# The row factor of an RMSNorm moved behind the up projection, with splits made tile by tile and up weights combined in place

## The chip, the cores and the metric

The kernel runs on one core of a Trainium2 chip. The metric is the device time of one execution in microseconds (us). The engines are named as in the profile: PE (TensorE matmul), PEld (its weight loads), DVE (VectorE), ACT (ScalarE), POOL (GpSimd) and SP (SyncE, which here only issues DMAs).

## The reference, cut to what matters

The model is a two-layer decoder trunk over 1032 rows (1024 of a prompt, 8 samples) with 1024 columns. Each layer adds a mixer's output through an output projection and then a convolutional FFN:

```python
x = x + jnp.concatenate([main, mo], axis=-1) @ prm['w_out'][l]
hn = _rmsnorm(x, prm['norm_ffn_g'][l])          # x * r * g, r one number per row
u = hn @ prm['w_ffn_up'][l]                     # 1024 -> 2 * 3072
u, nbuf = _causal_dwconv(u, buf, cw, cb)        # width 3, per channel
x = x + (jax.nn.gelu(u[..., :D_FF]) * u[..., D_FF:]) @ prm['w_ffn_down'][l]
```

All is float32. The row factor `r` is one number per row of `x`, so it can be applied to `hn` or, as well, to the rows of `u`.

## The kernel before, in words

Activations lie transposed: channels on the 128 partitions, the 1032 rows of the model along the free dimension. `row()` gives one tile of 128 x 1032 from a pool of 44, `sm()` one of 128 x 392 from a pool of 12. Every matrix product is done as three matmuls (`mm3`) on operands split in a high part (`fp32r`, copied by ACT) and the rest (a subtraction on POOL or DVE). So each weight and each activation is split before PE can use it. The order of ACT's instructions is the program's from the start up to the first layer's end and again in the last FFN (`act_in_order`); DVE, POOL, PE and SP are ordered by the compiler's scheduler. DMAs are all issued by SP, whose queue runs in order.

**Output projection** (`out_proj`). The 1032 columns are two halves of 516, each half two quarters of 258 (`QB`, `QW`). For each half the loop goes over the 8 output tiles `m`; each takes a split weight tile (`get`, one split ahead, one load ahead), loads the residual tile `x[m]` (first half), runs 2 x 24 matmuls, adds the result to `x[m]` on DVE, stores it to `rD` (SP), squares it on ACT and sums the squares on DVE (`on_tile`). Background work is a list of generators; `tick()` advances each by one step.

**Entry to the FFN** (`enter_ffn`). After each half `norm(hf)` computes the row factor (`inverse`: a matmul with ones, Ln and Exp on ACT, a correction step on DVE), multiplies every quarter of `x` by factor and gain (`scale`), and forms and splits the seven operands of a seven-product scheme (`B11`, `B21`, `B22`, `T1` to `T4`). The last half's `norm` runs after the last tile of the projection, and the products that follow need its results.

**Up projection** (`ffn`). For each of 24 channel pairs `j` there are seven products (`STEADY`), each 24 matmuls (12 for each half), with the weight combination made by `combine`, up to five products ahead: for a pair it makes 4 sums or differences of 128 x 512 and 7 splits of 128 x 512 on POOL, and 7 copies on ACT. Two of the sums stand in a row of their own (`S`). `load_pair(j + 1)` is asked for at the pair's first combination. ACT or DVE adds each product into the rows `ug`, `uv`. `post(j)` then makes the convolution: an ACT instruction (`act_conv`), two DVE taps for each row, an addition of 8 sample columns for each row (`taps`), a gelu on ACT and a product on DVE, and a store to `gD`.

**Down projection.** It reads `gD` back, splits and multiplies; `refill` reads `x` back from `rD`.

Of the kernel before, what the change touches and what calls it, by code (L numbers as in the profile page):

```python
# [36 lines left out]
DCH = 6  # L37
NDC = KF // DCH
# [4 lines left out]
STEADY = ("P1", "P6", "P2", "P7", "P5", "P4", "P3")  # L43
ENTRY = tuple((0, p, (0,)) for p in STEADY) + tuple((0, p, (1,)) for p in ("P1", "P2", "P6", "P7", "P5", "P4", "P3"))
SEQUENCE = ENTRY + tuple((j, p, (0, 1)) for j in range(1, KF) for p in STEADY)
ORDER_A = ("g2", "g3", "x0", "x1", "x2", "x3", "x4", "x5", "g4", "g5")
# [3 lines left out]
def tile_trunk(ctx: ExitStack, tc: tile.TileContext, I: dict, O: list):  # L50
# [502 lines left out]
    def unspill(k):  # L553
        t = row()
        SY.dma_start(t[:, :SEQ].rearrange("p (i t) -> p i t", i=8), xD[0:8, :, k, :].rearrange("i p t -> p i t"))
        SY.dma_start(t[:, SEQ:NT], xD[8, :, k, :NB])
        return t
# [132 lines left out]
    def sample_mem(l, dst):  # L690
# [35 lines left out]
        yield  # L726
        t = ps()
# [40 lines left out]
    def residual(l, m):  # L768
        if l:
            return unspill(m)  # L770
        t = row()
        SY.dma_start(t[:, :NT], I["x_t"][:, m, :])
        return t

    def out_proj(l, mget, ks, x, on_tile, on_half):
        for hb in range(2):
            for m in range(KD):
# [4 lines left out]
                for q in (2 * hb, 2 * hb + 1):  # L782
                    c0 = QB[q]
# [15 lines left out]
    def ffn_prep(l):  # L799
# [11 lines left out]
        vtt(s3, s3, c3, add)  # L811

    def up_weights(l):
# [10 lines left out]
        def combine(j, name):  # L824
            R = raws[j]
            lo_, hi_ = slice(0, 512), slice(512, 1024)
            if name == "P1":
                if j:
                    load_pair(j + 1)
                src = R["G"][:, lo_]  # L830
            elif name == "P6":
                S = R["S"] = row()
                gtt(S[:, lo_], R["V"][:, lo_], R["V"][:, hi_], add)
                gtt(S[:, hi_], S[:, lo_], R["G"][:, lo_], sub)
                src = S[:, hi_]
            elif name == "P2":
                src = R["G"][:, hi_]
            elif name == "P7":
                src = R["G"][:, lo_]
                gtt(src, src, R["V"][:, lo_], sub)  # L840
            elif name == "P5":
                src = R["S"][:, lo_]
            elif name == "P4":
                src = R["V"][:, hi_]
            else:
                src = R["S"][:, hi_]
                gtt(src, R["G"][:, hi_], src, sub)
# [4 lines left out]
            R["n"] = R.get("n", 0) + 1  # L852
            if R["n"] == 7:
                raws[j] = None
# [3 lines left out]
    def ffn(l, x, ops, need, weights, on_block, store=None):  # L858
# [5 lines left out]
        def act_conv(u, t):  # L864
            a = row()
            act(a[:, :NT], u[:, :NT], AF.Identity, scale=fwc(2, t), bias=fbc(t))
            G.tensor_copy(out=ul3[:, :, t], in_=u[:, SEQ - 2 : NT])
            return a

        def taps(a, u, t):  # L870
            stt(a[:, 1:SEQ], u[:, 0 : SEQ - 1], fwc(1, t), a[:, 1:SEQ], mul, add)
            stt(a[:, 2:SEQ], u[:, 0 : SEQ - 2], fwc(0, t), a[:, 2:SEQ], mul, add)
            vtt(a[:, SEQ:NT], a[:, SEQ:NT], sb3[:, :, t], add)

        def post(j):
# [9 lines left out]
            act(ag[:, :NT], ag[:, :NT], AF.Gelu_apprx_tanh)  # L885
            yield
            vtt(ag[:, :NT], ag[:, :NT], av[:, :NT], mul)
            SY.dma_start(gD[l, j], ag[:, :NT])
            yield

# [61 lines left out]

        last = []
        todo = [(0, p) for p in STEADY] + [(j, p) for j, p, _ in SEQUENCE if j]
        at = 7
        for q, (j, name, hfs) in enumerate(SEQUENCE):
            if q == 6:
                load_pair(1)
            want = 7 if q < 10 else min(len(todo), q - 7 + AHEAD)
# [51 lines left out]
        for b in range(3):  # L1011
            for m in range(KD):
                down(c, m, b)
                if store is not None:
                    store(m, b)
                tick()
            on_block(b)
# [269 lines left out]
    SY.dma_start(O[1], yl)  # L1287
    SY.dma_start(O[2], rl)
# [21 lines left out]
    def enter_ffn(l, x, mh, ml):  # L1310
        ops, gen, sums = {}, {}, {}

        def split(name, kk, hf, pair, raw, on_pool):
            hi, lo = pair
            acopy(hi, raw)
            (gtt if on_pool else vtt)(lo, raw, f(hi), sub)
            ops[name, kk, hf] = pair

        def cols(q):
            return slice(QB[q], QB[q] + QW)  # L1320

        def on_tile(q, m):
            SY.dma_start(rD[l, m, :, cols(q)], x[m][:, cols(q)])
            if m == 0:
                sums[q] = sm()
                act(sums[q][:, :QW], x[m][:, cols(q)], AF.Square)
            else:
                t = sm()
                act(t[:, :QW], x[m][:, cols(q)], AF.Square)
                vtt(sums[q][:, :QW], sums[q][:, :QW], t[:, :QW], add)  # L1330

        def inverse(q):
            a = sums.pop(q)
            p = ps()
            T.matmul(p[:, :QW], ones, a[:, :QW], start=True, stop=True)
            m, out, t = sm()[:, :QW], sm()[:, :QW], sm()[:, :QW]
            ts(V, m, p[:, :QW], 1.0 / D, EPS, mul, add)
            act(out, m, AF.Ln)
            act(out, out, AF.Exp, scale=-0.5)
            stt(t, m, -0.5, out, mul, mul)  # L1340
            vtt(t, t, out, mul)
            stt(out, t, 1.5, out, add, mul)
            return out

        def norm(hf):
            qa, qb = cols(2 * hf), cols(2 * hf + 1)
            ra, rb = inverse(2 * hf), inverse(2 * hf + 1)
            yield
            xs = lambda k, part: x[k][:, part]

            def scale(k, part, r):
                stt(xs(k, part), xs(k, part), g_ffn[l][k], r, mul, mul)

            def slot(k, part):
                return mh[k][:, part], ml[k][:, part]

            def own(n):
                for i in range(n):
                    if i % 2 == 0:
                        t = row(F32R)  # L1360
                    b = (i % 2) * 2 * QW
                    yield t[:, b : b + QW], t[:, b + QW : b + 2 * QW]

            for k in range(KD):
                scale(k, qa, ra)
                split("B11" if k < 4 else "B21", k % 4, hf, slot(k, qa), xs(k, qa), k % 2)
                if k % 4 == 3:
                    yield
            t2 = own(4)
            for kk in range(4):  # L1370
                scale(kk, qb, rb)
                scale(kk + 4, qb, rb)
                vtt(xs(kk, qa), xs(kk, qb), xs(kk, qa), sub)
                vtt(xs(kk, qb), xs(kk + 4, qb), xs(kk, qb), sub)
                split("B22", kk, hf, slot(kk + 4, qb), xs(kk + 4, qb), True)
                vtt(xs(kk + 4, qb), xs(kk + 4, qb), xs(kk, qa), sub)
                split("T2", kk, hf, next(t2), xs(kk + 4, qb), False)
                if kk % 2:
                    yield
            t2 = own(4)  # L1380
            for kk in range(4):
                split("T3", kk, hf, next(t2), xs(kk, qb), kk % 2)
            yield
            for kk in range(4):
                split("T1", kk, hf, slot(kk, qb), xs(kk, qa), kk % 2)
                if hf:
                    x[kk] = None
            yield
            t2 = own(4)
            for kk in range(4):  # L1390
                vtt(xs(kk + 4, qa), xs(kk + 4, qa), xs(kk + 4, qb), sub)
                split("T4", kk, hf, next(t2), xs(kk + 4, qa), kk % 2)
                if hf:
                    x[kk + 4] = None
            yield
# [3 lines left out]
        def first_pair():  # L1399
# [3 lines left out]
            yield  # L1403
            for name in STEADY:
                weights[1](0, name)
                yield

        def on_half(hf):
            if hf:
                finish(gen["w"])  # L1410
            gen[hf] = start(norm(hf))
            if not hf:
                gen["w"] = spawn(first_pair())
# [5 lines left out]
        return on_tile, on_half, need, ops, weights  # L1419
# [5 lines left out]

    x = [None] * KD
    ot, oh, need, ops, uw = enter_ffn(0, x, Mh, Ml)
    out_proj(0, mgetA, ks_a, x, ot, oh)
    Mh, Ml = {}, {}

# [52 lines left out]
    def handB(b, x=x):  # L1483
# [30 lines left out]
    ffn(0, x, ops, need, uw, handB)  # L1514
# [333 lines left out]
    x = [None] * KD  # L1848
# [5 lines left out]
    ot, oh, need, ops, uw = enter_ffn(1, x, Mh, Ml)  # L1854
# [3 lines left out]
    def y_out(m, b, x=x):  # L1858
# [133 lines left out]
```

## Time and profile before

| | |
|---|---|
| median of three runs | 2533.51 us (2530.58 to 2537.18) |
| profiled execution, its own time | 2532.97 us |
| its span in the trace | 2531.2 us |
| PE busy | 2336.5 us (92%) |
| mean granted TensorE clock | 0.964 of full |

The span is what lies between the first and the last recorded instruction; 1.8 us of the profiled execution's time lie around it. "Busy" of an engine includes time in which an instruction has begun and waits inside (for a port). Wait lists say which engine or DMA ended an idle time.

### The profile page before, as it was taken

To read this page: it belongs to the slowest core of one execution; us is meant where nothing else is said; L and a number is where in the kernel's file an instruction comes from. 1 tells how busy PE (TensorE), PEld (TensorE's weight loads), DVE (VectorE), ACT (ScalarE), POOL (GpSimd) and SP (SyncE) were. 2 spreads that over 40 slices of the span, in tenths; PEclk is the share of its full clock that TensorE was granted. 3 is DMA by queue.
4 is the path that set the end of the run, shared out by engine and by line. 5 is a ranking of instruction groups with operands and counts; after the bars stand their busy time and mean duration, and the time that the engine had idled before them with its cause. 6 is when DMAs were issued, how large, how long until landed. Compare 5 with 4: busy or idle time off the path is not lost. (4 is left out here: it accounts for less than half of the span.)

```text
span 2531.2 us, 42857 instructions
## 1 busy us (share of the span) xinstructions
PE 2336.5 (92%) x16590; PEld 2251.5 (89%) x16590; DVE 1549.6 (61%) x2826; ACT 1103.5 (44%) x2277; POOL 1428.0 (56%) x1123
## 2 busy tenths in 40 slices
PE   7997877799999999999989988787999999999999
PEld 5896866799999999999977787677999999999999
DVE  6658955666666666332478789875666566663321
ACT  5567753344433444211365577643443444442110
POOL 2149843588888885322144346435888888853220
PEclk9998989899999999999999999899999999999999
DMA  4221124212222225421575543551222222253311
GB/s 163 87 69 56 58 83 143 63 67 84 84 85 76 76 76 199 150 95 52 178 252 162 185 152 129 163 157 63 77 86 82 76 76 76 76 224 123 101 55 63
DMA packets 142491, 273.64 MB, mean 108 GB/s; under 512 B 28544, under 2 KB 85456, under 8 KB 142288
## 3 DMA queue, kind: packets, MB, share of 16 engines
q1 hardware_dynamic: 142288, 270.91, 31.9%
q8 instruction: 130, 2.13, 0.3%
q14 instruction: 73, 0.60, 0.1%
HBM read 211.99 MB, written 58.87 MB: 107 GB/s over the span
## 5 line engine op out<-in xcount | busy, mean ns | idle before, releaser
L116 POOL TENSOR_TENSOR row<-row,row 128x512 fp32r<-128x512 f32 (+9 forms) x754 | 1153.8, 1552 | 793.9 <-ACT row L105 476.4
L298 PE MATMUL ps<-row,row 128*128 128x258 f32 (+4 forms) x5032 | 1510.4, 303 | 55.5 <-ACT row L105 45.7
L299 PE MATMUL ps<-row,row 128*128 128x258 f32 (+4 forms) x5032 | 1509.1, 302 | 22.5 <-DVE row L113 18.7
L300 PE MATMUL ps<-row,row 128*128 128x258 f32 (+4 forms) x5032 | 1472.7, 301 | 23.5 <-POOL row L116 23.5
L298 PEld LDWEIGHTS ps<-row,row 128*128 128x128 f32 x5032 | 962.3, 191 | 73.9 <-ACT row L105 51.0
L299 PEld LDWEIGHTS ps<-row,row 128*128 128x128 f32 x5032 | 964.0, 192 | 40.2 <-DVE row L113 24.3
L300 PEld LDWEIGHTS ps<-row,row 128*128 128x128 f32 x5032 | 948.4, 192 | 34.1 <-POOL row L116 27.1
L105 ACT ACTIVATE row<-row 128x512 fp32r<-128x512 f32 (+8 forms) x768 | 505.4, 696 | 911.7 <-POOL row L116 305.4
L113 DVE TENSOR_TENSOR row<-row,ps 128x258 f32<-128x258 f32 (+2 forms) x736 | 322.3, 444 | 706.0 <-PE ps L300 666.5
L119 DVE SCALAR_TENSOR_TENSOR row<-row,fw,row 128x1023 f32<-128x1023 f32 x192 | 266.9, 1409 | 67.3 <-ACT row L105 67.3
L113 DVE TENSOR_TENSOR row<-row,row 128x258 fp32r<-128x258 f32 (+8 forms) x262 | 232.9, 912 | 31.3 <-ACT row L105 18.0
L105 ACT ACTIVATE row<-ps 128x258 f32<-128x258 f32 (+6 forms) x430 | 157.5, 406 | 69.6 <-PE ps L300 25.8
L116 POOL TENSOR_TENSOR row<-row,ty 128x768 f32<-128x768 f32 (+2 forms) x56 | 77.2, 1378 | 155.1 <-DVE ty L413 51.3
L105 ACT ACTIVATE row<-row,fw 128x1032 f32<-128x1032 f32 x96 | 114.9, 1245 | 68.8 <-DVE row L113 68.7
L105 ACT ACTIVATE sm<-row 128x258 f32<-128x258 f32 (+3 forms) x130 | 54.5, 452 | 153.5 <-DVE row L113 127.2
L113 DVE TENSOR_TENSOR row<-row,sb 128x8 f32<-128x8 f32 x96 | 102.3, 1066 | 0.0
L113 DVE TENSOR_TENSOR sm<-sm,sm 128x258 f32<-128x258 f32 (+5 forms) x125 | 81.9, 660 | 28.2 <-ACT sm L105 25.7
L105 ACT ACTIVATE row<-ps,ty,ty 128x256 f32<-128x256 f32 (+1 forms) x160 | 87.4, 564 | 10.1 <-DVE ty L113 7.6
L105 ACT ACTIVATE sm<-ps 128x384 f32<-128x384 f32 (+5 forms) x156 | 65.0, 444 | 39.2 <-PE ps L431 21.6
L113 DVE TENSOR_TENSOR row<-ps,row 128x384 fp32r<-128x384 f32 (+2 forms) x125 | 63.5, 519 | 25.1 <-ACT row L105 10.2
L119 DVE SCALAR_TENSOR_TENSOR row<-sm,pack,row 128x384 f32<-128x384 f32 (+1 forms) x54 | 62.6, 1162 | 14.6 <-POOL row L124 13.3
L116 POOL TENSOR_TENSOR sm<-sm,row 128x192 f32<-128x192 f32 (+3 forms) x72 | 49.5, 702 | 36.1 <-ACT sm L105 18.6
(163 smaller groups left out, 1497.3 us busy)
## 6 DMA issues: line engine op xcount, KB each, us to landing
row<-in_w_ffn_up SPq DMA_DIRECT2D x96, 512.0 KB, 3.3
gD<-row SPq DMA_DIRECT2D x48, 516.0 KB, 2.6
row<-gD SPq DMA_DIRECT2D x48, 516.0 KB, 5.6
row<-in_w_ffn_down SPq DMA_DIRECT2D x64, 384.0 KB, 3.1
row<-hD SPq DMA_DIRECT2D x48, 512.0 KB, 6.6
row<-in_w_out SPq DMA_DIRECT2D x32, 512.0 KB, 4.2
rD<-row SPq DMA_DIRECT2D x64, 129.0 KB, 1.9
row<-rD SPq DMA_DIRECT2D x16, 516.0 KB, 8.7
```

The source lines that it names most:

```text
L105: return nc.scalar.activation(out, in_, func, **kw)
L113: return V.tensor_tensor(out=out, in0=a, in1=b, op=op)
L116: return G.tensor_tensor(out=out, in0=a, in1=b, op=op)
L119: return V.scalar_tensor_tensor(out=out, in0=a, scalar=s, in1=b, op0=op0, op1=op1)
L298: T.matmul(out, ah, bh, start=first and j == 0, stop=False, skip_group_check=more)
L299: T.matmul(out, ah, bl, start=False, stop=False, skip_group_check=more)
L300: T.matmul(out, al, bh, start=False, stop=last and j == n - 1, skip_group_check=more)
```

## The change

- `out_proj` goes over the tiles in the order 0, 4, 1, 5, ... (`TILES`), and residual tiles hold a half of two channel tiles; they are asked for ahead of the loop and then one for each of the first four tiles of a half.
- `on_tile` adds on DVE into a small tile, copies that times the gain into `x` on ACT, and stores the small tile to `rD` by a DMA issued on ACT's queue. The sums and splits of `T2`, `T3`, `T4` (`combine_x`) are made after every second tile; `settle` splits `B11` with `T1`, and `B21` with `B22`, as rows of 516.
- The row factor is not applied there. `factor()` makes one row `rf` in the middle of the first products, and `act_conv` multiplies each finished row `ug`, `uv` (128 x 1032) by it on DVE, 96 times in all.
- The 8 sample columns leave `taps`; `samples` treats them for 12 pairs at a time, with POOL, and stores them apart.
- `combine` works in the raw weight rows in the order `PREPARED`; the row `S` is gone; the next pair is asked for at `P4`, the sixth of seven. The first pair's combinations begin in the first half of the projection.
- Two small outputs are stored after the projection of layer 0 instead of ahead of it, and the sample attention over memory has two more `yield`s between its softmax and its transposes.

```diff
-            for m in range(KD):
+            for m in TILES:
                 key = f"out{l}.{hb}.{m}"
                 wh, wl = get(key, 1, 1)
-                if x[m] is None:
-                    x[m] = residual(l, m)
+                if m < 4:
+                    fetch()
...
-                    vtt(x[m][:, c0 : c0 + QW], x[m][:, c0 : c0 + QW], p[:, :QW], add)
-                    on_tile(q, m)
+                    on_tile(hb, part, m, p[:, :QW])
...
         def combine(j, name):
-            if name == "P1":
-                if j:
-                    load_pair(j + 1)
-                src = R["G"][:, lo_]
+            if name == "P1":
+                src = G[:, lo_]
+            elif name == "P7":
+                src = G[:, lo_]
+                gtt(src, src, V_[:, lo_], sub)
             elif name == "P6":
-                S = R["S"] = row()
-                gtt(S[:, lo_], R["V"][:, lo_], R["V"][:, hi_], add)
-                gtt(S[:, hi_], S[:, lo_], R["G"][:, lo_], sub)
-                src = S[:, hi_]
+                src = G[:, lo_]
+                gtt(src, V_[:, hi_], src, sub)
...
+            if name == "P4" and j:
+                load_pair(j + 1)
...
         def act_conv(u, t):
+            vtt(u[:, :NT], u[:, :NT], factor()[:, :NT], mul)
             a = row()
-            act(a[:, :NT], u[:, :NT], AF.Identity, scale=fwc(2, t), bias=fbc(t))
+            act(a[:, :SEQ], u[:, :SEQ], AF.Identity, scale=fwc(2, t), bias=fbc(t))
...
         def taps(a, u, t):
-            vtt(a[:, SEQ:NT], a[:, SEQ:NT], sb3[:, :, t], add)
...
+        def on_tile(hf, part, m, p):
+            q = 2 * hf + part
+            xs, t = place(hf, part, m), sm()
+            vtt(t[:, :QW], xs, p, add)
+            acopy(xs, t[:, :QW], scale=g_ffn[l][m])
+            nc.scalar.dma_start(rD[l, m, :, QB[q] : QB[q] + QW], t[:, :QW])
...
+        def combine_x(hf, kk):
+            a, b = place(hf, 0, kk), place(hf, 1, kk)
+            c, d = place(hf, 0, kk + 4), place(hf, 1, kk + 4)
+            t3, t2, t4 = (sm()[:, :QW] for _ in range(3))
+            vtt(t3, d, b, sub)
+            vtt(b, b, a, sub)
+            vtt(t2, d, b, sub)
+            vtt(t4, c, t2, sub)
...
+        def settle(hf):
+            cs = slice(hf * HALF, hf * HALF + HALF)
             for kk in range(4):
+                for a, names in enumerate((("B11", "T1"), ("B21", "B22"))):
+                    k = kk + 4 * a
+                    hi, lo, raw = mh[k][:, cs], ml[k][:, cs], x[hf, kk][:, a * HALF : a * HALF + HALF]
+                    acopy(hi, raw)
+                    (gtt if a else vtt)(lo, raw, f(hi), sub)
```

## Rows read from the trace of the kernel before

**Rows 1.** The page: busy time of each engine over the span.
```profile
PE 2336.5 (92%) x16590; PEld 2251.5 (89%) x16590; DVE 1549.6 (61%) x2826; ACT 1103.5 (44%) x2277; POOL 1428.0 (56%) x1123
```

**Rows 2.** Windows: two projection-and-entry stretches, one up-projection slice, layer 0's up projection.
```profile
347.20:522.40 175.20, 132.05 (x926) 125.18 (x927) 98.98 (x187) 61.90 (x142) 85.00 (x67) 0.87 0.33 106
1660.00:1785.80 125.80, 98.02 (x696) 92.33 (x695) 83.36 (x170) 49.09 (x117) 63.81 (x57) 0.88 0.27 85
...
700.00:800.00 100.00, 100.00 (x835) 100.00 (x834) 63.88 (x85) 42.06 (x70) 85.08 (x65) 1.00 0.23 80
...
523.00:985.00 462.00, 459.65 (x3819) 459.06 (x3818) 297.90 (x390) 195.25 (x322) 389.88 (x295) 1.00 0.23 82
```

**Rows 3.** PE's waits, 345 to 523 us: total, times, longest.
```profile
PE ps L298 <- ACT row L105: 20.1, 9, 8.2
PE ps L300 <- POOL row L116: 12.4, 9, 2.0
```

**Rows 4.** SP's queue in time: start, us, line, transfer.
```profile
344.77 0.34 SPq L1287 DMA_DIRECT2D out<-yl  x1
...
366.67 0.80 SPq L1323 DMA_DIRECT2D rD<-row  x2
...
1671.54 32.45 SPq L1323 DMA_DIRECT2D rD<-row  x10
1704.09 0.37 SPq L251 DMA_DIRECT2D row<-in_w_out  x1
```

**Rows 5.** DVE's waits, 345 to 412 us.
```profile
DVE row L113 <- DMA row<-in_x_t: 37.4, 7, 6.0
```

**Rows 6.** Groups of the whole kernel by shape: one POOL split, the scaling on DVE.
```profile
L116 POOL TENSOR_TENSOR row<-row,row 128x1024 fp32r<-128x1024 f32 x46 | 114.7, 2495 | 110.8 <-ACT row L105 92.3 <-issue 13.4 <-DMA rD<-row 5.1
...
L119 DVE SCALAR_TENSOR_TENSOR row<-row,pack,sm 128x258 f32<-128x258 f32 x64 | 39.2, 672 | 0.2
```

**Rows 7.** PE's waits, 200 to 345 us: the longest.
```profile
PE ps L729 <- DVE sm L123: 12.6, 1, 12.6
```

**Rows 8.** POOL's groups by shape, 600 to 900 us, fifteen pairs.
```profile
L116 POOL TENSOR_TENSOR row<-row,row 128x512 fp32r<-128x512 f32 x105 | 165.3, 1592 | 44.8 <-ACT row L105 44.8
L116 POOL TENSOR_TENSOR row<-row,row 128x512 f32<-128x512 f32 x45 | 73.0, 1622 | 0.0
L116 POOL TENSOR_TENSOR row<-row 128x512 f32<-128x512 f32 x15 | 19.4, 1295 | 0.0
```

**Rows 9.** DVE's groups by shape, 600 to 900 us.
```profile
L113 DVE TENSOR_TENSOR row<-row,sb 128x8 f32<-128x8 f32 x30 | 37.8, 1260 | 0.0
...
L113 DVE TENSOR_TENSOR row<-row,row 128x1032 f32<-128x1032 f32 x15 | 18.3, 1222 | 0.0
```

**Rows 10.** DVE in time, part of one pair, and one early addition.
```profile
525.73 0.16 DVE L113 TENSOR_TENSOR row<-row,sb 128x8 f32<-128x8 f32 x1
...
669.11 1.27 DVE L119 SCALAR_TENSOR_TENSOR row<-row,fw,row 128x1023 f32<-128x1023 f32 x1
...
671.49 1.27 DVE L119 SCALAR_TENSOR_TENSOR row<-row,fw,row 128x1022 f32<-128x1022 f32 x1
...
673.87 0.41 DVE L113 TENSOR_TENSOR row<-row,ps 128x258 f32<-128x258 f32 x1
674.54 1.22 DVE L113 TENSOR_TENSOR row<-row,row 128x1032 f32<-128x1032 f32 x1
```

**Rows 11.** POOL in time, the same pair.
```profile
658.02 1.29 POOL L116 TENSOR_TENSOR row<-row 128x512 f32<-128x512 f32 x1
659.26 1.30 POOL L116 TENSOR_TENSOR row<-row,row 128x512 fp32r<-128x512 f32 x1
...
669.26 2.27 POOL L116 TENSOR_TENSOR row<-row,row 128x512 fp32r<-128x512 f32 x1
674.52 2.38 POOL L116 TENSOR_TENSOR row<-row,row 128x512 fp32r<-128x512 f32 x1 [2.98 <-ACT row L105]
```

**Rows 12.** DMA issues: size, count, median us from issue to landing.
```profile
row<-in_w_ffn_up SPq DMA_DIRECT2D x96, 512.0 KB, 3.3
```

More of the change, by code (lines that the diff above doesn't have):

```diff
@@ L851, in combine, with ffn @@
             made[j, name] = w
-            R["n"] = R.get("n", 0) + 1
-            if R["n"] == 7:
+            if name == "P4" and j:
+                load_pair(j + 1)
+            if name == "P3":
                 raws[j] = None
         return load_pair, combine, made
-    def ffn(l, x, ops, need, weights, on_block, store=None):
+    def ffn(l, ops, need, factor, weights, on_block, store=None):
         ul3 = ul.rearrange("p (c t) -> p c t", c=10)
@@ L951, in refill @@
             SY.dma_start(x[m][:, :NT], rD[l, m])
+        x = [None] * KD
         last = []
-        todo = [(0, p) for p in STEADY] + [(j, p) for j, p, _ in SEQUENCE if j]
+        todo = [(j, p) for j in range(KF) for p in PREPARED]
         at = 7
@@ L958, in ffn @@
                 load_pair(1)
+            if q == 10:
+                factor()
             want = 7 if q < 10 else min(len(todo), q - 7 + AHEAD)
@@ L1310, in enter_ffn, with split @@
     def enter_ffn(l, x, mh, ml):
-        ops, gen, sums = {}, {}, {}
-        def split(name, kk, hf, pair, raw, on_pool):
-            hi, lo = pair
+        ops, gen, sums, own, wait = {}, {}, {}, {}, []
+        rf = []
+        def split(name, kk, hf, hi, lo, raw):
             acopy(hi, raw)
[L1316 to L1323, printed above, removed]
+            vtt(lo, raw, f(hi), sub)
+            ops[name, kk, hf] = hi, lo
@@ L1327, in on_tile @@
             else:
[L1328 to L1369, printed above, removed]
-            for kk in range(4):
[L1371 to L1395, printed above, removed]
@@ new lines, in on_tile @@
+                s = sm()
+                act(s[:, :QW], t[:, :QW], AF.Square)
+                vtt(sums[q][:, :QW], sums[q][:, :QW], s[:, :QW], add)
+            if part == 0 and wait:
+                combine_x(*wait.pop())
+            if part == 1 and m >= 4:
+                wait.append((hf, m - 4))
+        def combine_x(hf, kk):
[6 more added lines that the diff above has]
+            vtt(t4, c, t2, sub)
+            for name, t in (("T3", t3), ("T2", t2), ("T4", t4)):
+                if kk % 2 == 0:
+                    own[name] = row(F32R)
+                o = (kk % 2) * HALF
+                split(name, kk, hf, own[name][:, o : o + QW], own[name][:, o + QW : o + HALF], t)
@@ new lines, in inverse @@
+        def inverse():
+            rf.append(row())
+            for q in range(4):
+                a = sums.pop(q)
+                p = ps()
+                T.matmul(p[:, :QW], ones, a[:, :QW], start=True, stop=True)
+                m, t, r = sm()[:, :QW], sm()[:, :QW], a[:, :QW]
+                ts(V, m, p[:, :QW], 1.0 / D, EPS, mul, add)
+                act(r, m, AF.Ln)
+                act(r, r, AF.Exp, scale=-0.5)
+                stt(t, m, -0.5, r, mul, mul)
+                vtt(t, t, r, mul)
+                stt(rf[0][:, QB[q] : QB[q] + QW], t, 1.5, r, add, mul)
@@ L1402, in first_pair @@
             yield
-            yield
-            for name in STEADY:
+            for name in PREPARED:
                 weights[1](0, name)
                 yield
+        gen["w"] = spawn(first_pair())
         def on_half(hf):
+            if wait:
+                combine_x(*wait.pop())
             if hf:
                 finish(gen["w"])
-            gen[hf] = start(norm(hf))
-            if not hf:
-                gen["w"] = spawn(first_pair())
+            gen[hf] = start(settle(hf))
         def need(name, kk, hf):
@@ L1417, in need, with factor @@
                 advance(gen[hf])
-        return on_tile, on_half, need, ops, weights
+        def factor():
+            if not rf:
+                inverse()
+            return rf[0]
+        return on_tile, on_half, need, ops, weights, factor
     def mgetA(k, c0, n):
```

117 lines of the change are left out of this document (81 added, 36 removed).

## The prediction

> **What bounds the kernel now.** I read the page's busy times first: PE is busy for 92% of the span, no other engine for more than 61% [rows 1]. That is a mean over unlike stages, so I cut the span into windows [rows 2]. In layer 0's up projection PE is busy for 459.7 of 462 us, at full clock, and a slice of it has 835 matmuls in 100 us, which is 0.1198 us each; layer 1's is alike. Nothing can be won there. In the two stretches from an output projection to the end of the first pair's products it is otherwise: layer 0's has 926 matmuls in 175.2 us, layer 1's 696 in 125.8 us. At 0.1198 us these need 110.9 and 83.4 us, so 64.3 and 42.4 us are lost, 106.7 us together; part of it by the clock, which the windows give as 0.87 and 0.88.
>
> The wait lists say who PE waited for there: splits by ACT (20.1 us) and POOL (12.4 us) [rows 3]. Behind them stand queues. In layer 0's first half DVE waits 37.4 us for the residual tile, 7 times [rows 5], since its load stands in SP's queue behind the store of the tile before; ahead of all, the store of `yl` holds the queue until 344.8 us. In layer 1's second half SP spends 32 us on ten `rD` stores, each waiting for DVE, and only then asks for the next weight, at 1704.1 us [rows 4].
>
> **What the change takes from these stretches.** The residual is asked for ahead and the stores leave SP's queue, so both waits go. The factor and gain on DVE (64 x 0.672 = 43 us [rows 6]) go; the gain becomes an ACT copy. The operand splits are spread over the projection, so that after its last tile only the last pair of tiles and the second half's `settle` are left, behind seven products that have their operands.
>
> What stays lost, estimated: in layer 0 the second column block's split, 4 us; POOL's queue in the first half, where eleven operations of the first pair (11 x 1.25 = 13.8 us) now meet the weight splits of 2.5 us each [rows 6], four of them in the same seven quarters (20 us of PE) and the mixer's splits before them, 12 us; second half, 2 us; the entry with `settle`, the factor's ones-matmuls and their DVE chain, 9 us. That is 27 us. In layer 1 there is no mixer split on POOL: 6 + 2 + 9 = 17 us. The gain is 106.7 - 44 = **63 us**. Bounds: 40 us if POOL's queue costs twice as much, 87 us if only the first split and the entry's matmuls stay. The stores that ACT now issues: no row shows ACT's issue; SP's takes 0.40 us each (0.80 for two [rows 4]), so 32 x 0.40 = 12.8 us in a stretch in which ACT is busy for 61.9 of 175.2 us [rows 2]; hidden, at worst some 10 us over both projections. The softmax's two yields may fill PE's wait of 12.6 us [rows 7], bounds 0 to 12.6; DVE is the busier engine there, so I take 2 us.
>
> **What it costs in the up projections.** DVE gains two multiplications of 128 x 1032 for each pair and loses two additions of 8 columns. By busy time that is nothing: 1.222 against 1.260 us each [rows 9]. But 1.26 us for 8 columns is no work: the same addition took 0.16 us at 525.7 us, when it did not have to wait [rows 10]. What it waits for is POOL. POOL's split that begins 0.15 us after a DVE tap takes 2.27 us, the one beside the product of 1032 columns takes 2.38 us, and undisturbed ones follow each other in 1.25 us [rows 10, 11]. So while DVE works on two inputs of SBUF POOL stands still, and the other way round: these instructions take turns.
>
> I count the turns of one pair. POOL: 165 operations in fifteen pairs are 11 [rows 8], at 1.25 us 13.8 us. DVE: four taps, two in 2.38 us (671.49 to 673.87), and one product, 1.2 us each, 6.0 us [rows 10]. With the two 10-column copies this is nearly the whole pair of 20.1 us (168 x 0.1198). Followed along the clock, the only time in the pair in which neither holds the turn is from 673.87 to 674.52, 0.65 us [rows 10, 11]. POOL's idle of 2.98 us before 674.52 is no slack, as DVE's two last taps lie in it.
>
> The change adds 2 x 1.19 us of turns and takes away 2 x 0.08: 2.2 us a pair where 0.65 are free. So a pair needs at least 20.1 + 1.57 us. I take 2.1, since the handover through ACT (gelu) that leaves the 0.65 free stays. 22 pairs in each layer prepare a successor, 44 in all; weights are made some three to four products ahead of use, from which I let 5 us a layer be absorbed. Cost: 44 x 2.1 - 10 = **82 us**; lower bound 44 x 1.57 - 10 = 59 us if all of the turn is used.
>
> The Trainium skill has this in "SBUF — State Buffer", section "Who interferes with whom": a DVE instruction with two SBUF inputs and a GpSimd instruction that reads SBUF exclude each other, and the second stands still for the whole of the first. Taken with whole recorded durations (1.29 us for POOL, 1.27 and 1.22 for DVE), the pair before would already need some 21.2 us; the trace shows 20.1, so it agrees in kind and the turn is shorter than the record. By the rule the pair after would be some 3.2 us longer than 20.1, and the cost 131 us, the time about 2599 us; it is counted with rival (b).
>
> **The rest.** The combinations in place are still 11 POOL operations a pair; each must now wait until ACT has copied what it overwrites, where `S` let two run ahead. This is four handovers through ACT where there were three, and it falls on an engine that has no time: nothing below, up to 1 us a pair above, held in the upper bound. The later request: two products, 5.7 us, lie between `P4` and the first use, and such a load lands in 3.3 us [rows 12]; the rows are freer without `S`, so nothing. The samples in twelves: a few short POOL operations, nothing. ACT's 1024 instead of 1032 columns: nothing. The last pair's two multiplications lie beside the first down matmuls: nothing. If the cover of the load is gone, `P1` is late and PE waits for its first split.
>
> **Sum.** 2533.0 (the profiled execution's own time, 1.8 us over its span, and 0.5 us under the median) - 63 - 2 + 82 = **2550 us**.
>
> **Rivals.**
> (a) *The turns don't bind*: POOL's 2.98 us idle takes up the multiplications, and PE stays at 20.1 us a pair. For it: POOL is 85% busy, and the busy sums of DVE are equal. Against: the 8 columns that last 1.26 us. Time: 2533 - 65 = **2468 us**; with half of the cost, 2509. It ends faster than before. It decides where a pair lengthens by less than 75/44 = 1.7 us at the gain of 65 us and the lead of 10: that is close to my lower bound, so a well-packed port or a larger gain brings it about too.
> (b) *The chain gets long*: ACT runs in order, and its first instruction of `post` now waits for a multiplication, its gelu for taps that come later; behind it stand the copies of the next weights and the eviction of `P1`. POOL then keeps its idle of 2.98 us on top of the turns: 17.2 us busy, + 2.4 blocked, + 2.98 + handovers of 1 us = 23.6 us a pair. Cost 44 x 3.5 - 10 = 144 us: 2533 - 65 + 144 = **2612 us**.
> (c) *The stretches don't shorten*: POOL or the rows (more weights, T rows and raws beside the sliding-window attention's in layer 1) hold PE as long as before, gain 20 us: 2533 - 22 + 82 = **2593 us**.
>
> **How the numbers follow.** My forecast has a chance of 0.45, (a) 0.30, (b) 0.15, (c) 0.10. A measurement of this kernel tells about 0.3%, 7.6 us, from no change. The forecast's own range, with gain 50 to 80 and cost 59 to 100, is 2512 to 2583; of its 0.45, 0.10 lie under 2526 and 0.09 within 0.3%. Faster: 0.30 + 0.10 = 0.40; same 0.09, say 0.10; slower 0.50. The whole range leaves out the ends of (a) and (b): 2474 to 2610.
>
> **What would show it.** Right: windows in the up projections with PE near 90 to 93% and fewer than 780 matmuls in 100 us; multiplications of 128 x 1032 on DVE recorded at well over 1.22 us, or POOL's 512-column operations at a mean over 1.7 us; the pair's period at 21.7 to 22.5 us; the two stretches shorter by 50 to 80 us in all; no DVE wait for the residual, no `rD` store on SP. Wrong: a pair of still 20.1 us (then the turns are not what I take them for), or stretches of the old length.

## The result, and the profile after

The kernel after takes 2603.88 us (median of four runs, 2596.87 to 2605.24) against 2534.89 us of the kernel before beside it (2530.58 to 2537.18): the ratio is 1.0269, 95% interval 1.0245 to 1.0292. The change makes the kernel 2.7% slower; the forecast was 2550 us.

To see where the time goes, the stores to `gD` serve as marks, one for each channel pair. The rows are DMA groups of SP, one for each layer; the two times are the first and the last start. Before:

```profile
L888 SPq DMA_DIRECT2D gD<-row x24: 319/327/327, 534.7 to 1000.8; - x24
L888 SPq DMA_DIRECT2D gD<-row x24: 320/326/327, 1797.6 to 2263.4; - x24
```

After:

```profile
L912 SPq DMA_DIRECT2D gD<-row x24: 319/326/483, 500.4 to 1021.5; - x24
L912 SPq DMA_DIRECT2D gD<-row x24: 320/326/382, 1816.6 to 2336.4; - x24
```

They cut the span in five. The same marks were read in every run:

| kernel | to layer 0's first store | its 23 further pairs | to layer 1's first store | its 23 further pairs | rest | span |
|---|---|---|---|---|---|---|
| before | 534.7 | 466.1 | 796.8 | 465.8 | 267.8 | 2531.2 |
| after | 500.4 | 521.1 | 795.1 | 519.8 | 267.1 | 2603.5 |
| 1: after, no multiplication | 498.4 | 485.6 | 796.7 | 470.7 | 265.1 | 2516.5 |
| 2: after, factor in PSUM | 498.4 | 496.2 | 791.9 | 501.4 | 264.9 | 2552.8 |
| 3: before, multiplication by ones | 533.7 | 508.2 | 804.6 | 508.8 | 267.8 | 2623.1 |
| 4: before, new combinations | 538.0 | 492.2 | 804.8 | 492.0 | 267.8 | 2594.8 |
| 5: as 4, request at `P1` | 537.0 | 491.4 | 800.6 | 492.2 | 267.7 | 2588.9 |
| 6: after, old combinations | 499.7 | 507.2 | 791.5 | 503.7 | 265.5 | 2567.6 |
| 7: after, third block early | 501.4 | 519.6 | 784.7 | 517.7 | 267.2 | 2590.6 |
| 8: PSUM, old combinations, POOL's 8 columns | 496.9 | 468.6 | 789.7 | 467.8 | 264.8 | 2487.8 |
| 9: as 4, results apart | 531.2 | 474.2 | 800.5 | 473.4 | 267.7 | 2547.0 |
| 10: as 8, third block early | 498.4 | 468.5 | 779.4 | 468.6 | 264.8 | 2479.7 |
| 11: as 8, new combinations | 495.5 | 495.6 | 791.4 | 500.2 | 265.5 | 2548.2 |
| 12: as 10, without the yields | 498.2 | 468.2 | 780.1 | 468.5 | 264.8 | 2479.8 |

So the change gains 34.3 us up to layer 0's first pair, 1.7 us in the stage that holds layer 1's projection and 0.7 us behind, 36.7 us in all. It pays 55.0 and 54.0 us, 109.0 us, in the up projections: a pair takes 22.6 us where it took 20.3.

The windows of after (busy time, instructions and PE's clock; [rows 2] has those of before):

```profile
700.00:800.00 100.00, 93.73 (x755) 92.36 (x754) 62.90 (x76) 34.41 (x58) 80.00 (x63) 0.98 0.20 70
...
600.00:900.00 300.00, 278.98 (x2236) 274.53 (x2235) 200.74 (x224) 113.57 (x190) 252.48 (x181) 0.98 0.20 71
```

There are 755 matmuls instead of 835 in 100 us. PE now waits, and its waits (600 to 900 us) name POOL's splits:

```profile
PE ps L303 <- POOL row L119: 19.1, 12, 4.4
PE ps L301 <- ACT row L108: 1.6, 2, 0.9
```

POOL's groups in the same window, and DVE's group of the multiplication ([rows 8, 9] have the groups of before):

```profile
L119 POOL TENSOR_TENSOR row<-row,row 128x512 fp32r<-128x512 f32 x94 | 152.3, 1640 | 41.3 <-ACT row L108 41.3
L892 POOL COPY ul<-row 128x10 f32<-128x10 f32 x28 | 19.2, 710 | 2.8 <-DVE row L116 2.8
...
L116 DVE TENSOR_TENSOR row<-row,row 128x1032 f32<-128x1032 f32 x27 | 41.1, 1522 | 1.9
```

The group of the copies in the kernel before:

```profile
L867 POOL COPY ul<-row 128x10 f32<-128x10 f32 x30 | 6.0, 200 | 0.0
```

A multiplication of 128 x 1032 took 1222 ns for the product of `post` before [rows 9], and takes 1522 now; a copy of ten columns took 200 ns on POOL, and takes 710. These are waits inside the instructions. But POOL is also idle for 41.3 us behind ACT, while PE waits for POOL.

The 23 intervals of a layer aren't alike. The one behind the 12th store, where `samples` treats its first twelve pairs with five POOL operations, lasts 26.2 us in both layers, some 4 us more than the others. Layer 0's 12th and 13th store, the five operations, and PE's wait in 744 to 772 us:

```profile
744.32 0.33 SPq L912 DMA_DIRECT2D gD<-row  x1
770.50 0.33 SPq L912 DMA_DIRECT2D gD<-row  x1
```

```profile
741.16 1.70 POOL L119 TENSOR_TENSOR sm<-ul,fw 128x96 f32<-128x96 f32 x2
742.83 1.71 POOL L119 TENSOR_TENSOR sm<-sm,sb 128x96 f32<-128x96 f32 x2
...
746.96 0.41 POOL L119 TENSOR_TENSOR sm<-sm,sm 128x96 f32<-128x96 f32 x1
```

```profile
PE ps L303 <- POOL row L119: 4.4, 1, 4.4
```

The last interval of a layer, with the second twelve, is longer too (27.0 and 26.8 us for 22.8 before). The other 21 take 22.3 us on average, where they took 20.1.

In layer 0's projection the waits that were to go are gone: no DVE wait for the residual tile [rows 5], and the 32 `rD` stores are ACT's, 0.326 us each at the median.

### The profile page after: what moved, and what is told of

It is laid out like the page before. It is cut to its first block, busy times and chain, and to the rows that moved or that the text cites. A ratio compares the mean times of both kernels' runs of the same rounds, so it can differ in the third digit from the quotient of the medians.

```text
span 2603.5 us, 42803 instructions
## 1 busy us (share of the span) xinstructions
PE 2366.6 (91%) x16590; PEld 2273.8 (87%) x16590; DVE 1652.1 (63%) x2772; ACT 1123.4 (43%) x2313; POOL 1492.1 (57%) x1103
## 5 line engine op out<-in xcount | busy, mean ns | idle before, releaser
L119 POOL TENSOR_TENSOR row<-row,row 128x512 fp32r<-128x512 f32 (+9 forms) x666 | 1071.4, 1623 | 783.6 <-ACT row L108 483.1
L302 PEld LDWEIGHTS ps<-row,row 128*128 128x128 f32 x5032 | 970.3, 193 | 39.0 <-DVE row L116 22.3
L108 ACT ACTIVATE row<-row 128x512 fp32r<-128x512 f32 (+9 forms) x688 | 482.9, 737 | 930.7 <-POOL row L119 436.2
L116 DVE TENSOR_TENSOR row<-row,ps 128x258 f32<-128x258 f32 (+2 forms) x672 | 294.1, 446 | 625.9 <-PE ps L303 620.0
L116 DVE TENSOR_TENSOR row<-row,row 128x1032 f32<-128x1032 f32 (+8 forms) x286 | 361.8, 1277 | 38.7 <-ACT row L108 22.6
L122 DVE SCALAR_TENSOR_TENSOR row<-row,fw,row 128x1023 f32<-128x1023 f32 x192 | 317.9, 1714 | 73.1 <-ACT row L108 73.1
L108 ACT ACTIVATE row<-row,fw 128x1024 f32<-128x1024 f32 x96 | 114.1, 1237 | 92.4 <-DVE row L116 92.4
L119 POOL TENSOR_TENSOR row<-row 128x512 f32<-128x512 f32 x96 | 146.9, 1530 | 3.8
L108 ACT ACTIVATE sm<-ps 128x384 f32<-128x384 f32 (+5 forms) x156 | 65.0, 444 | 38.7 <-PE ps L434 21.5
L892 POOL COPY ul<-row 128x10 f32<-128x10 f32 x96 | 69.1, 742 | 14.9 <-DVE row L116 14.9
L122 DVE SCALAR_TENSOR_TENSOR row<-sm,pack,row 128x384 f32<-128x384 f32 (+1 forms) x54 | 59.8, 1111 | 14.0 <-POOL row L127 12.7
```

Of the source, the lines that this page charges most:

```text
L108: return nc.scalar.activation(out, in_, func, **kw)
L116: return V.tensor_tensor(out=out, in0=a, in1=b, op=op)
L119: return G.tensor_tensor(out=out, in0=a, in1=b, op=op)
L122: return V.scalar_tensor_tensor(out=out, in0=a, scalar=s, in1=b, op0=op0, op1=op1)
L302: T.matmul(out, ah, bl, start=False, stop=False, skip_group_check=more)
```

## Theories and experiments

Theory 1: the multiplications take turns with POOL, as the prediction had it. Theory 2: the combinations made in place cost POOL time, since each has to wait until ACT has copied what it overwrites. Theory 3: the next pair's request comes too late. Theory 4: the length of the chain through ACT, and not the turns, is the cost. The experiments are numbered as they ran and told by cause. "Loss" is what the 46 pair intervals of the two layers take above the kernel before; like the table it is read from one profiled execution of each kernel. Ratios are to the kernel before, run beside each.

**1. No multiplication** (the kernel after; the row factor is left out of the result).

```diff
         def act_conv(u, t):
-            vtt(u[:, :NT], u[:, :NT], factor()[:, :NT], mul)
```

> The kernel after without the two multiplications of u by the row factor for each pair; the factor is made but left out of the result. Theory 1 (the multiplications take turns with POOL) and theory 4 (they lengthen the chain through ACT) expect a pair at 20.1 to 20.4 us, 463 to 470 us from layer 0's first gD store to its last (521.1 after, 466.1 before), and a time of about 2495 to 2500 us. Theory 2 (the combinations in place) and theory 3 (the later request) expect the pair to stay above 22 us and the time at 2590 us or more. Values between say that both have a part.

2517.4 us, 0.9949 (0.9932 to 0.9966), between the two expectations. 84.6 us of the 109.0 in the pairs go, and 24.4 stay, 19.5 of them in layer 0. The multiplications are the larger part; they aren't all of it. What stays is uneven: layer 0's first 14 intervals take 21.2 to 22.0 us each, its later ones and layer 1's mostly 20.0 to 20.1, as before. Why some pairs pay and others don't was not found.

**2. Factor in PSUM.** Two banks hold the factor's 1024 columns, a small tile its last 8.

```diff
-            vtt(u[:, :NT], u[:, :NT], factor()[:, :NT], mul)
+            fa, fb, fc = factor()
+            vtt(u[:, :512], u[:, :512], fa[:, :512], mul)
+            vtt(u[:, 512:SEQ], u[:, 512:SEQ], fb[:, :512], mul)
+            vtt(u[:, SEQ:NT], u[:, SEQ:NT], fc[:, :NB], mul)
...
+            full, fa, fb, fc = rf.pop(), ps(), ps(), ty()
+            V.tensor_copy(out=fa[:, :512], in_=full[:, :512])
+            V.tensor_copy(out=fb[:, :512], in_=full[:, 512:SEQ])
+            V.tensor_copy(out=fc[:, :NB], in_=full[:, SEQ:NT])
```

> The kernel after with the row factor kept in two PSUM banks (1024 columns) and a small tile (8 columns): each multiplication becomes two of 512 columns and one of 8, with one SBUF and one PSUM input in the large ones. Theory 1 (turns between two SBUF inputs on DVE and POOL) expects a pair at 20.1 to 20.6 us, POOL's 512-column operations near the 1.25 to 1.45 us they take undisturbed, and 2495 to 2525 us. Theory 4 (the chain through ACT is longer by what the multiplication lasts, whatever its inputs) expects 22 us or more a pair and 2590 to 2605 us, since the multiplication is not shorter.

2557.1 us, 1.0110 (1.0095 to 1.0125): between the two expectations. DVE's groups of the new instructions:

```profile
L116 DVE TENSOR_TENSOR row<-row,ps 128x512 f32<-128x512 f32 x56 | 37.1, 684 | 3.3 <-DVE row L116 0.5
...
L116 DVE TENSOR_TENSOR row<-row,ty 128x8 f32<-128x8 f32 x28 | 19.1, 684 | 0.5
```

With one input in PSUM 512 columns take 684 ns (as in experiments 8 and 11), and 8 columns with both inputs in SBUF take as long, though the kernel before has one of 0.16 us [rows 10]. So the 8 columns wait, as those of the kernel before did beside POOL. They were to be dealt with too, and the other 30 and 36 us in the pairs had to be split further.

**3. The multiplication alone**, added to the kernel before, by a row of ones.

```diff
         def act_conv(u, t):
+            vtt(u[:, :NT], u[:, :NT], one[:, :NT], mul)
             a = row()
```

> The kernel before with one thing added: each finished up row is multiplied on DVE by a row of ones, 128 x 1032, two SBUF inputs, two for each pair. Theories 1 and 4 expect nearly the whole cost of the change from this alone: a pair at 22.1 to 22.7 us and 2533 + 44 x 2.0 to 2.4 = 2620 to 2640 us. Theories 2 and 3 expect the time of before within 8 us.

2621.4 us, 1.0366 (1.0351 to 1.0382), as theories 1 and 4 say. The pairs grow by 42.1 and 43.0 us, 85.1 us, from the first pair on. PE's waits in 600 to 900 us are now many short ones:

```profile
PE ps L298 <- ACT row L105: 8.0, 13, 0.7
PE ps L300 <- POOL row L116: 7.6, 13, 0.6
```

**4. The combinations alone**, in the kernel before: in place, new order, request at `P4`, no `S`, no multiplication.

```diff
-            elif name == "P6":
-                S = R["S"] = row()
-                gtt(S[:, lo_], R["V"][:, lo_], R["V"][:, hi_], add)
-                gtt(S[:, hi_], S[:, lo_], R["G"][:, lo_], sub)
-                src = S[:, hi_]
+            elif name == "P7":
+                src = G[:, lo_]
+                gtt(src, src, V_[:, lo_], sub)
+            elif name == "P6":
+                src = G[:, lo_]
+                gtt(src, V_[:, hi_], src, sub)
...
+            if name == "P4" and j:
+                load_pair(j + 1)
```

> The kernel before with the combinations of the change alone: made in the raw weight rows in the new order, the next pair asked for at P4, no row S, no multiplication. Theories 1 and 4 expect the time of before within 8 us and a pair of 20.1 to 20.3 us. Theories 2 and 3 expect 22 us or more a pair and 2620 to 2640 us. A small part of the cost here (0.3 us a pair, 13 us) would show as 2545.

2589.5 us, 1.0242 (1.0222 to 1.0262). Theories 1 and 4 expected no change here; they fall as the only cause. Theories 2 and 3 expected 22 us or more a pair; it is 21.4. 26.1 and 26.2 us are lost in the pairs, 1.1 us each. POOL's waits in 600 to 900 us, before:

```profile
POOL row L116 <- ACT row L105: 44.8, 15, 3.0
```

With the new combinations:

```profile
POOL row L117 <- ACT row L106: 64.6, 34, 4.3
```

POOL in time, one pair of it (start, duration, count; in brackets the idle time before and who ended it):

```profile
664.81 6.26 POOL L117 TENSOR_TENSOR row<-row,row 128x512 fp32r<-128x512 f32 x4 [2.98 <-ACT row L106]
671.15 1.30 POOL L117 TENSOR_TENSOR row<-row 128x512 f32<-128x512 f32 x1
672.40 1.31 POOL L117 TENSOR_TENSOR row<-row,row 128x512 fp32r<-128x512 f32 x1
673.65 0.21 POOL L867 COPY ul<-row 128x10 f32<-128x10 f32 x1
673.80 1.30 POOL L117 TENSOR_TENSOR row<-row,row 128x512 f32<-128x512 f32 x1
675.84 2.55 POOL L117 TENSOR_TENSOR row<-row,row 128x512 fp32r<-128x512 f32 x2 [0.74 <-ACT row L106]
...
685.98 6.25 POOL L117 TENSOR_TENSOR row<-row,row 128x512 fp32r<-128x512 f32 x4 [2.98 <-ACT row L106]
```

The idle time of 2.98 us that the kernel before has in every pair is still there, and a second one of 0.74 us is new: POOL has made a combination, has nothing else that it may do, and stands until ACT has copied it. From 664.81 to 685.98 us is 21.17 us for one pair. (In 3 and 4 the stage up to layer 1's first store is 8 us longer too; why was not looked into.)

**5. The request at `P1` again**, the rest as in 4.

```diff
             if name == "P1":
+                if j:
+                    load_pair(j + 1)
                 src = G[:, lo_]
...
-            if name == "P4" and j:
-                load_pair(j + 1)
```

> The kernel before with the combinations made in place in the new order, but the next pair's weights asked for at P1 as before. The same with the request at P4 lasted 2589.5 us, its pair 21.4 us. Theory 2 (in place, each combination waits until ACT has copied what it overwrites, and POOL stands idle meanwhile) expects 21.2 to 21.5 us a pair and 2580 to 2592 us, with POOL's short waits of 0.75 us for ACT still there. Theory 3 (the later request is late) expects 20.3 us a pair and 2530 to 2540 us.

2590.9 us, 1.0242 (1.0225 to 1.0260); pairs 21.4 us, POOL waits 32 times for ACT. Theory 3 falls.

**9. The results apart**: as 4, but the results of `P7` and `P6` go to a row of their own.

```diff
             elif name == "P7":
-                src = G[:, lo_]
-                gtt(src, src, V_[:, lo_], sub)
+                S = R["S"] = row()
+                src = S[:, lo_]
+                gtt(src, G[:, lo_], V_[:, lo_], sub)
             elif name == "P6":
-                src = G[:, lo_]
-                gtt(src, V_[:, hi_], src, sub)
+                src = R["S"][:, hi_]
+                gtt(src, V_[:, hi_], R["S"][:, lo_], sub)
```

> The kernel before with the new order of the combinations and the request at P4, but the results of P7 and P6 written to a row of their own instead of over the raw weights, so that neither waits for ACT's copy of what it overwrites. In place the pair took 21.4 us and the kernel 2589.5 us. If the wait for the overwritten half is the cost, the pair falls to 20.2 to 20.5 us and the time to 2530 to 2545 us. If it is the new order (four results that POOL makes, ACT copies and POOL at once needs back, one after the other), the pair stays at 21.2 to 21.5 us and the time at 2578 to 2595 us.

2549.7 us, 1.0071 (1.0056 to 1.0086), just above both upper bounds of the first expectation. The pairs' loss falls from 52.3 to 15.7 us: 36.6 us came from `P7` and `P6` writing over the raw weights, 15.7 us from what else is new (`P3` still writes over the half that ACT copies for `P2`). POOL waits for ACT 21 times:

```profile
POOL row L117 <- ACT row L106: 54.4, 21, 4.3
```

**6. The old combinations in the kernel after**; the multiplications stay. The edit is the one of 4, reversed.

> The kernel after with the combinations as before the change: row S, the old order, the request at P1; the multiplications stay. Without the multiplications, the rest of the change still cost 19.5 us in layer 0 and 4.9 us in layer 1. If the parts add (theory 1 with theory 2), a pair falls to 21.6 to 22.1 us and the time to 2550 to 2580 us. If the multiplications alone fill POOL's time and the handovers lie in their shadow, the pair stays above 22.3 us and the time at 2592 us or more.

2564.6 us, 1.0131 (1.0114 to 1.0148). The pairs' loss falls from 109.0 to 79.0 us. So in the kernel after the two parts nearly add: 79.0 here without the new combinations and 24.4 in experiment 1 without the multiplications make 103.4. The 12th intervals, those of `samples`, last 25.9 us here, beside 21.7 and 21.5 us of the others; 8.6 us of the 79.0 are theirs.

**8. Both causes taken away**: the old combinations, the factor in PSUM, and POOL multiplies the 8 sample columns in the 10-column copy that it makes anyway (`fc` begins with two ones).

```diff
-            vtt(u[:, SEQ:NT], u[:, SEQ:NT], fc[:, :NB], mul)
...
-            G.tensor_copy(out=ul3[:, :, t], in_=u[:, SEQ - 2 : NT])
+            gtt(ul3[:, :, t], u[:, SEQ - 2 : NT], fc[:, : NB + 2], mul)
```

> The kernel after with the row factor in two PSUM banks, the combinations as before the change, and the 8 sample columns multiplied by POOL in the 10-column copy it makes anyway, so that DVE has no added instruction with two SBUF inputs. Theory 1 with theory 2 (turns and handovers are all of the cost) expects a pair at 20.2 to 20.7 us and 2493 to 2515 us, below the kernel before. Theory 4 (ACT's convolution starts later by what the multiplication lasts, whatever its inputs) expects 21.2 us a pair or more and 2535 us or more.

2490.4 us, 0.9841 (0.9827 to 0.9856): faster than both kernels, and a little under the first expectation. The pairs take 20.4 us, 4.5 us in all above the kernel before, nearly all of it in the last interval of each layer; the 12th take 20.0 and 19.9 us. The windows, POOL's groups and POOL's waits in 600 to 900 us:

```profile
600.00:900.00 300.00, 300.00 (x2499) 300.00 (x2498) 210.36 (x283) 126.09 (x211) 241.12 (x199) 1.00 0.23 78
```

```profile
L119 POOL TENSOR_TENSOR row<-row,row 128x512 f32<-128x512 f32 x45 | 57.6, 1295 | 0.0
...
L119 POOL TENSOR_TENSOR ul<-row,ty 128x10 f32<-128x10 f32 x30 | 5.8, 213 | 0.3 <-DVE row L116 0.3
```

```profile
POOL row L119 <- PE ps L303: 30.4, 15, 2.2
POOL row L119 <- ACT row L108: 28.0, 14, 2.1
```

Eight splits run through on POOL at 1.26 us each while DVE multiplies from PSUM (four multiplications and three additions of matmul results):

```profile
679.39 10.06 POOL L119 TENSOR_TENSOR row<-row,row 128x512 fp32r<-128x512 f32 x8
```

```profile
685.43 4.02 DVE L116 TENSOR_TENSOR row<-row,ps 128x258 f32<-128x258 f32 x7 [1.98 <-PE ps L303]
```

PE is never idle, and POOL waits for PE in every pair: 30.4 us of POOL's idle time are now slack, since the rows that it wants to fill are still in use. DVE is busier (210 us) than in the kernel after (201) and it costs nothing. The multiplication still stands ahead of ACT's convolution in the chain, and lasts nearly as long (2 x 684 ns), so theory 4 falls for this order of the combinations.

**11. As 8, with the combinations of the change.**

> The kernel after with the factor in two PSUM banks and the 8 sample columns multiplied by POOL in its 10-column copy, the combinations as in the change. With the 8 columns as an instruction of DVE with two SBUF inputs it lasted 2557 us; without any multiplication 2517 us. Theory 1 (turns between two SBUF inputs and POOL) expects the multiplications to cost nearly nothing then: 2512 to 2525 us. Theory 4 (ACT's convolution starts later by what they last) expects 2545 to 2560 us.

2557.1 us, 1.0105 (1.0086 to 1.0124): theory 4's expectation, no better than experiment 2. The groups of POOL show where:

```profile
L119 POOL TENSOR_TENSOR ul<-row,ty 128x10 f32<-128x10 f32 x28 | 23.8, 849 | 7.0 <-DVE row L116 7.0
```

In experiment 8 POOL comes to these copies late, behind eight 512-column operations; here it comes to them early. They wait 7.0 us for the multiplication, and last 849 ns in place of 213. The long ones lie inside DVE's four taps, and a short one behind such a wait:

```profile
678.52 6.53 DVE L122 SCALAR_TENSOR_TENSOR row<-row,fw,row 128x1023 f32<-128x1023 f32 x4 [0.77 <-POOL row L119]
```

```profile
679.29 1.20 POOL L119 TENSOR_TENSOR ul<-row,ty 128x10 f32<-128x10 f32 x1
...
701.28 0.21 POOL L119 TENSOR_TENSOR ul<-row,ty 128x10 f32<-128x10 f32 x1 [1.73 <-DVE row L116]
```

With the new combinations PSUM saves 45.1 us (109.0 to 63.9), with the old ones 74.5 us (79.0 to 4.5). Between the 63.9 us here and the 24.4 us without any multiplication 39.5 us are left, which the multiplications cost here even out of PSUM. How much of them is POOL's and ACT's waiting for the multiplication, and how much the copies that now meet the taps, no run separates.

**7 and 10. The third column block of layer 1's mixer earlier**, in the kernel after and in the one of 8.

```diff
+                if l and (hb, m) == (0, 1):
+                    start_m(2)
                 if m < 4:
                     fetch()
```

> The kernel after, with the mixer's third column block in layer 1's output projection asked for after the first tile instead of at the start of the second half. If PE's wait of 12.7 us near 1712 us comes from these loads standing in SP's queue behind the residuals of the second half and weights that wait for rows, the stretch from layer 0's last gD store to layer 1's first falls from 795 us to 780 to 787 us and the time by 8 to 14 us, to 2590 to 2596 us. If rows or POOL hold the projection anyway, the wait moves and the time stays within 5 us of 2604 us.

> The fastest so far (factor in PSUM, old combinations, sample columns on POOL: 2490.4 us) with the third column block in layer 1 asked for after the first tile. In the kernel after this edit took 10.4 us from the stretch between layer 0's last gD store and layer 1's first. If the wait is there too, 2478 to 2484 us; if in the faster kernel the rows come free in another order and the loads are not late, within 4 us of 2490 us.

2599.5 us (2592.4 to 2600.8) for 7, ratio 1.0267 (1.0250 to 1.0283); 2486.8 us (2481.5 to 2489.5) for 10, ratio 0.9820 (0.9804 to 0.9836). In both profiles the stage is some 10 us shorter (795.1 to 784.7, 789.7 to 779.4), but both profiled executions are the fastest of their four. The medians fall by 4.4 and 3.6 us, which the spread of the runs doesn't tell from nothing; by the time alone both lie within the bounds that their expectations gave for no gain. So what the edit is worth isn't shown. What is plain is the wait. SP's loads of `mD` and PE's waits from 1700 to 1740 us, after:

```profile
L1854 SPq DMA_DIRECT2D row<-mD x20: 359/467/1342, 1645.3 to 1717.8; - x20
```

```profile
PE ps L301 <- ACT row L108: 12.7, 1, 12.7
PE ps L302 <- DVE row L116: 1.2, 1, 1.2
```

Experiment 7:

```profile
L1856 SPq DMA_DIRECT2D row<-mD x20: 359/465/601, 1644.3 to 1679.3; - x20
```

```profile
PE ps L303 <- POOL row L119: 3.1, 3, 1.3
```

In the kernel after these loads stand in SP's queue behind residual tiles of the second half and weights that wait for rows. Asked for earlier, the last is issued at 1679.3 instead of 1717.8 us, and the wait of 12.7 us is gone from here (one of 5.3 us stays at 1680 to 1700 us). Part of it moves: from the last store of `qsD` to layer 1's first store to `gD`, PE's waits for ACT's rows fall from 27.1 to 20.4 us only (from 23.9 to 14.0 us in experiment 10); in the kernel before they are 15.7 us.

**12. Without the two yields**, the rest as in 10.

```diff
         ts(V, pt[:32, :256], pt[:32, :256], rd[:32, :1], None, mul, None)
         yield
-        yield
-        yield
```

> The fastest so far (2486.8 us: factor in PSUM, old combinations, sample columns on POOL, the third column block early) without the two added yields between the sample softmax and its transposes. The prediction gave the yields 2 us, with bounds of 0 and 12.6 us from PE's one long wait in layer 0. If they fill that wait, it is back and the first gD store comes 8 to 13 us later, 2492 to 2500 us in all. If they only push the sample attention into the next stage of layer 1, where the way from the loads of kvD to the last store of qsD grew by 2 to 7 us with the change, it shrinks again and the time is 2480 to 2486 us. If neither, within 3 us of 2486.8 us.

2484.4 us (2481.7 to 2490.5), ratio 0.9827 (0.9813 to 0.9841): the same; the time fits the second and the third expectation alike. PE's long wait is back, and it costs nothing (200 to 345 us):

```profile
PE ps L740 <- DVE sm L126: 12.6, 1, 12.6
PE ps L301 <- ACT row L108: 6.6, 1, 6.6
```

With the yields PE waits there for other things instead:

```profile
PE ps L301 <- ACT sm L108: 15.0, 8, 4.6
PE ps L774 <- DVE row L116: 6.1, 1, 6.1
```

## Why the prediction was right in sign and wrong in size

The forecast was 2550 us and the profiled execution's own time 2605.2 us, 55 us more. In the terms of its sum, 27 us of that are cost (109.0 for 82) and 28 us are gain that did not come (36.7 for 65). Two terms make up nearly all of it: the combinations (30 us for nothing) and layer 1's stretch (1.7 us for 25).

- **The multiplications' turns: right in kind and, with the old combinations, in size.** 82 us were forecast, 59 as lower bound. Measured: 85.1 us alone (experiment 3), 79.0 us in the kernel after with the old combinations (6). The 10 us that were to be absorbed are not seen in experiment 3, where a pair loses 2.0 us from the first on; that 82 is so near 85.1 is in part luck. The signs in the up projections came as named: multiplication at 1522 ns, PE at 93%, 755 matmuls in 100 us. That it is turns and not work is shown by experiment 8: 1024 of the 1032 columns still on DVE, one input in PSUM, the other 8 on POOL, and 4.5 us are left. With the combinations of the change it is less plain: of the 84.6 us that go without the multiplications (1), PSUM gives back 45.1 (11). The rule of the Trainium skill in "SBUF — State Buffer", "Who interferes with whom", that a DVE instruction with at most one SBUF input, outside the 2-port modes, doesn't contend with GpSimd, agrees with the 684 ns for 512 columns and POOL's 1.26 us a split beside them (8). The Trainium skill's blocking for whole durations gave 131 us, and 85.1 was measured; that the time of 2599 us worked out from it is near the result is chance.
- **"The combinations in place: nothing below, up to 1 us a pair above": the step that failed.** The middle of the two bounds was not taken, but zero, although the same sentence counts four handovers through ACT instead of three, on an engine "that has no time". They cost 1.1 us a pair alone in the kernel before (52.3 us, experiment 4), 0.65 beside the multiplications (109.0 - 79.0 = 30.0 us over 46 pairs), and at most 24.4 us in the kernel after without them (1); why less there is open. Seven tenths of the 52.3 us is the writing of `P7` and `P6` over the raw weights (9). The later request costs nothing, as forecast (5).
- **"The samples in twelves: a few short POOL operations, nothing": wrong too, and small.** They are 3.8 us of POOL's time twice a layer. Where POOL sets the pace the 12th interval is some 4 us longer than the others, 8 us in the two layers (they are part of the 79.0 above); in experiment 8, where POOL has slack, it isn't.
- **Layer 0's stretch: right.** 37 us and 2 for the yields were forecast, 34.3 came, 37.8 in experiment 8. The 2 us of the yields aren't there (12).
- **Layer 1's stretch: the other step that failed.** 25 us were forecast and 1.7 came. The step "in layer 1 there is no mixer split on POOL: 6 + 2 + 9 = 17 us" left out that the residuals asked for ahead now stand in SP's queue before the mixer's third block; that wait is 12.7 us. Without it the stage is 12.1 us shorter than before (7), 17.4 with the faster pairs (10), by one profile each; the medians fall by some 4 us only. Some further microseconds go ahead of the projection: from the first load of `kvD` to the last store of `qsD` it is 249.0 us before and 253.7 after (250.9 in experiment 10, 249.4 in 12, so the yields are 1.5 us of it at most). What does the rest wasn't found, nor where the 8 us between 17.4 and 25 are; so the cause of this miss is shown in part, and the rest is open.
- **The rivals.** (a), turns that don't bind, falls by experiment 3. (b) came nearest with 2612 us. Its 144 us are measured as 109.0. POOL did keep its idle time behind ACT (41.3 us in 300, some 3 us a pair), as (b) had it; but with the old combinations the multiplication ahead of ACT costs nearly nothing once the turns are gone (8). With the new ones up to 39.5 us are its cost (11), so (b) may have a part in the kernel as changed. (c) is half of it: the gain was 36.7 us where (c) had 22, and it failed in layer 1, as (c) had it, though by SP's queue.

## What to carry to other kernels

Work that is moved to an engine with free time isn't free if its instructions take turns with those of the engine that sets the pace. Here one input in PSUM took the turns away, and the same work cost 4.5 us in place of 79.0; but only with the old combinations, so try such a remedy together with the other edits of a change. Where an engine has as little time left as POOL here, writing a result over its source saves a row and costs a wait: count how far the engine may run ahead, not only its operations. On such an engine a few short operations cost what they last. And when loads are asked for earlier, list what stands behind them in the same queue: here the wait went to that.

## What the runs showed of the hardware

An operation of 8 or 10 columns takes as long as the instructions that it takes turns with let it: 10 columns on POOL lasted 213 ns in experiment 8 and 849 ns in 11, by the same instruction in another order. And busy time doesn't tell such waits from work. Experiments 6 and 8 have the same combinations and multiply the same rows; the windows of 6:

```profile
600.00:900.00 300.00, 282.32 (x2291) 277.78 (x2290) 209.77 (x233) 115.59 (x195) 264.37 (x184) 0.99 0.22 75
```

DVE is busy for 209.77 us there and for 210.36 in 8, with 233 instructions against 283, and PE for 282.32 us against 300.00.
